# Column mean of an 8192 x 8192 matrix: other early blocks, an earlier start for TensorE's sums, two GpSimd adds and stores from two queues

## The chip, the cores and the metric

The kernel runs on one core of a Trainium2 chip. The metric is device time in microseconds (us): the median of three runs. Engines are named as the profile names them: PE is TensorE, DVE is VectorE, ACT is ScalarE, POOL is GpSimd, SP is SyncE. Times inside the profiled execution are counted from the start of its span.

## The reference

```python
def setup_inputs():
    return {
        "x": np.random.randn(8192, 8192).astype(np.float32),
    }

def reference(x: np.ndarray) -> np.ndarray:
    return np.mean(x, axis=0)
```

The input is 268.4 MB, the output 32 KB.

## The kernel before

**Tiling.** The 8192 rows are G = 64 groups of 128 rows, so a group is a tile of 128 partitions by 8192 float32 (4096 KB). Columns are cut into 16 blocks of F = 512; the sixteenth block is cut once more into four quarters of W = 128. The sum over the 64 groups and 128 partitions is made in two stages: VectorE adds groups element by element into `acc`, and TensorE sums over the partitions by a matmul with a 128 x 32 tile `ones` that holds 1/8192, adding up in PSUM what it is given: `acc` and the last two groups (62 and 63), which VectorE never touches.

**Loads.** All are issued by SyncE, in program order, through `load` (L52). `early` (6 blocks wide) is filled with the first six blocks of group 61 (`load_early`, L88: two blocks at once, four more at g = 4). Groups come in pairs, 8192 KB per load (L98), into four buffers `bufs[:, 0:4]` (and the first pair into the two that become `both` and `acc`). After the loop come group 60, the last ten blocks of group 61, group 62, and group 63 in four pieces of 8, 4, 3 and 1 blocks (L117 to L122). A load that reuses a buffer waits for the VectorE add that read it.

**VectorE.** For each pair, one add makes `both` from the pair (L106) and one adds `both` to `acc` (L107); then group 60 (all 16 blocks, L117) and group 61 (its last ten blocks, L119) are added to `acc`. In `add` (L71) an add that waits for a load has its waits put on a no-op of another engine's queue, ScalarE's or GpSimd's (L75), and waits for that no-op alone.

**GpSimd** adds the six early blocks to `acc`, in two adds, after g = 24 and g = 32 (L111).

**TensorE.** `blocks` (L126) lists one matmul per block: block i goes to strip q = i % 4, that is output partitions 32q to 32q + 31 of PSUM tile `banks[i // 4]`; the quarters of block 15 go to the four strips of `last`. The order is fixed by hand: all of group 62, all of `acc`, all of group 63 (L135 to L137), 16 blocks each. In the profile each matmul stands as two records: 90 records for 45 blocks, 24 for 12 quarters.

**Output.** ScalarE copies the four banks to SBUF (L152), VectorE copies `last` to `tail` (L160), and SyncE stores: banks 0 to 2 in one store, bank 3 in a second, `tail` in a third (L164 to L166). `landed` (L46) makes SyncE wait for what must be over by the end.

Of the kernel before, what the change touches and what calls it, by code (L numbers as in the profile page):

```python
# [9 lines left out]
def kernel(  # L10
# [5 lines left out]
    nc = tc.nc  # L16
    f32 = mybir.dt.float32
    M, N = x.shape
    P = nc.NUM_PARTITIONS
    F = 512  # L20
    W = F // 4
    G = M // P
# [8 lines left out]
    acc = bufs[:, U - 1, :]  # L31
    ones = sb.tile([P, 32], f32, name="ones")
    E = 6
    early = sb.tile([P, E * F], f32, name="early")
# [6 lines left out]
    banks = [psp.tile([P, F], f32, name=f"bank{b}") for b in range(4)]  # L41
# [4 lines left out]
    def landed(*inss):  # L46

        nop = tc.keep_in_program_order(nc.sync.nop()).ins
        for o in inss:
            tc.add_manual_dep(nop, o.name, sync, reason="SyncE waits")  # L50

    def load(dst, src):  # L52
        ins = tc.keep_in_program_order(nc.sync.dma_start(out=dst, in_=src)).ins  # L53
        k = len(loads)
        over = loads[k - 8:k - 6] if k >= 8 and k % 2 == 0 else []
        tc.declare_no_dep(ins, group="loads", keep=over, reason="the reader of the buffer waited")
        for o in over:
            tc.add_manual_dep(ins, o.name, sync, reason="covers the next load too")
        tc.add_to_no_dep_group("loads", ins)
        loads.append(ins)  # L60
        return ins

    def rows(g, n=1):
        return x[g * P:(g + n) * P, :]
# [6 lines left out]
    def add(dst, a, b, dmas):  # L71

        ins = tc.keep_in_program_order(nc.vector.tensor_add(out=dst, in0=a, in1=b)).ins  # L73
        if dmas:
            waiter = nc.scalar if len(adds) % 8 > 1 else nc.gpsimd  # L75
            nop = joins[waiter] = tc.keep_in_program_order(waiter.nop()).ins  # L76
            for o in dmas + adds[-1:]:
                tc.add_manual_dep(nop, o.name, sync, reason="the no-op waits")
            for group in ("loads", "adds"):
                tc.declare_no_dep(ins, group=group, reason="the no-op waited")  # L80
            tc.add_manual_dep(ins, nop.name, sync, reason="waits for both at once")
        elif adds:
            tc.declare_no_dep(ins, group="loads", reason="the add ahead waited")
        tc.declare_no_dep(ins, group="early", reason="the no-op waited, or the add behind it")
        tc.add_to_no_dep_group("adds", ins)
        adds.append(ins)

    def load_early(lo, hi):  # L88
        load(early[:, lo * F:hi * F], rows(G - 3)[:, lo * F:hi * F])

    sums2 = bufs[:, U - 2:, :]
    load_early(0, 2)
    first = [load_rows(0, U - 2, 2)]
    tc.keep_in_program_order(nc.scalar.copy(out=warm[:], in_=ones[:]))  # L94
    ahead = []
    for g in range(2, G - 4, 2):
        u = (g + 2) % 4
        dma = load_rows(g, u, 2)  # L98
        if g < 6:
            add(sums2, sums2, bufs[:, u:u + 2, :], [dma] + first)  # L100
            first = []
            if g == 4:
                load_early(2, E)
                add(acc, acc, both, [])
            continue
        add(both, bufs[:, u, :], bufs[:, u + 1, :], [dma])  # L106
        add(acc, acc, both, ahead)  # L107
        ahead = []
        if g in (24, 32):
            cols = slice(0, 2 * F) if g == 24 else slice(2 * F, E * F)  # L110
            ins = tc.keep_in_program_order(nc.gpsimd.tensor_add(  # L111
                out=acc[:, cols], in0=acc[:, cols], in1=early[:, cols])).ins
            tc.add_to_no_dep_group("early", ins)
            ahead = [ins]

    r60, r61, r62, r63 = [bufs[:, (G - 4 + 2 + j) % 4, :] for j in range(4)]
    add(acc, acc, r60, [load(r60, rows(G - 4))])  # L117
    cols = slice(E * F, N)
    add(acc[:, cols], acc[:, cols], r61[:, cols], [load(r61[:, cols], rows(G - 3)[:, cols])])  # L119
    load(r62, rows(G - 2))  # L120
    for lo, hi in [(0, 8), (8, 12), (12, 15), (15, 16)]:
        load(r63[:, lo * F:hi * F], rows(G - 1)[:, lo * F:hi * F])  # L122

# [2 lines left out]
    def blocks(row, lo, hi):  # L126
        for i in range(lo, hi):
            if i < 15:
                sums.append((banks[i // 4], i % 4, row[:, i * F:(i + 1) * F]))
            else:  # L130
                for q in range(4):
                    at = i * F + q * W
                    sums.append((last, q, row[:, at:at + W]))

    blocks(r62, 0, 16)  # L135
    blocks(acc, 0, 16)
    blocks(r63, 0, 16)  # L137
    for n, (dst, q, cols) in enumerate(sums):
        summed = tc.keep_in_program_order(nc.tensor.matmul(  # L139
            out=dst[32 * q:32 * q + 32, :],  # L140
            lhsT=ones[:],
            rhs=cols,
            start=all((d is dst, k) != (True, q) for d, k, _ in sums[:n]),
            stop=all((d is dst, k) != (True, q) for d, k, _ in sums[n + 1:]),
            tile_position=(0, 32 * q),
            skip_group_check=True,
        )).ins

    res = both[:, :4 * F].rearrange("p (b c) -> p b c", b=4)

    def copy(dst, src):
        return tc.keep_in_program_order(nc.scalar.copy(out=dst, in_=src)).ins  # L152

    def store(engine, dst, src):
        return tc.keep_in_program_order(engine.dma_start(out=dst, in_=src)).ins

    for b in range(3):
        copy(res[:, b, :], banks[b][:])
    copied = copy(res[:96, 3, :], banks[3][:96])
    ended = nc.vector.tensor_copy(out=tail[:], in_=last[:]).ins  # L160
    landed(*joins.values())
    landed(loads[-5], set_up)
    landed(*loads[-4:-2])
    s0 = store(nc.sync, out[:12 * F].rearrange("(b q c) -> q b c", q=4, c=F), res[0:P:32, 0:3, :])  # L164
    s3 = store(nc.sync, out[12 * F:15 * F].rearrange("(q c) -> q c", q=3), res[0:96:32, 3, :])
    store(nc.sync, out[15 * F:].rearrange("(q c) -> q c", q=4), tail[0:P:32, :])  # L166
    landed(*loads[-2:])
    landed(copied, summed)
    landed(s0, ended)
    landed(s3)  # L170
    hold = tc.keep_in_program_order(nc.vector.nop()).ins
    tc.add_manual_dep(hold, s0.name, sync, reason="VectorE ends late")
# [30 lines left out]
```

## Time and profile before

| what | value |
|---|---|
| time, median of three runs (lowest to highest) | 631.97 us (631.57 to 632.15) |
| the profiled execution: its own time | 632.94 us |
| the profiled execution: its span | 630.8 us |
| HBM read / written | 268.44 MB / 0.03 MB, 426 GB/s over the span |
| busy in the span: DVE / PE / POOL / ACT | 529.8 / 14.0 / 7.4 / 3.8 us |
| group 62 and later loads issued by SyncE from | 596.14 us |
| TensorE's matmuls, first start to last end | 612.97 to about 627 us |

Sections of the page: 1 gives busy time by engine, 2 the span in 40 slices, 4 the chain of work that ended last, 5 groups of instructions by line. "SPq" and "ACTq" are the sequencers of SyncE and ScalarE; a DMA issue there is the time that the issuing takes, not the transfer. Over most of the span the DMA rows are full; the last 20 us are where the engines' order shows.

### The profile page before, as it was taken

The page shows a single profiled execution, that of the slowest core. Times are in us where ns is not written, and L with a number is a line of the kernel's source. Part 1 is how long each engine was busy: PE and PEld are TensorE (multiplying, and loading weights), DVE is VectorE, ACT ScalarE, POOL GpSimd, SP SyncE. Part 2 cuts the span into 40 slices and gives each one's busy share as a digit, 9 for nine tenths or more (in the row PEclk, how much of TensorE's full clock was granted, in tenths as well). Part 3 has the DMA queues.
Part 4 walks back from the last instruction along what each step waited for, and adds up shares of the span by engine and source line. Part 5 has one row for each costly group of instructions (what it writes and reads, how often), then busy time and mean ns, then how long its engine had stood idle before and what let it go on. Part 6 is the DMA issues. An engine that isn't in the chain of part 4 may idle for free.

```text
span 630.8 us, 448 instructions
## 1 busy us (share of the span) xinstructions
PE 14.0 (2%) x114; PEld 5.3 (1%) x114; DVE 529.8 (84%) x60; ACT 3.8 (1%) x6; POOL 7.4 (1%) x8
## 2 busy tenths in 40 slices
PE   0000000000000000000000000000000000000017
PEld 0000000000000000000000000000000000000002
DVE  0028999999888898888998899988889888889892
ACT  0000000000000000000000000000000000000001
POOL 0000000000000000010000200000000000000000
PEclk9999999999999999999999999999999999999999
DMA  9999999999999999999999999999999999999994
GB/s 387 445 449 390 479 411 461 403 465 399 465 399 465 399 465 399 465 399 465 399 465 411 453 420 445 441 424 449 416 461 403 461 403 465 399 465 399 422 430 182
DMA packets 5648, 268.50 MB, mean 426 GB/s; under 512 B 635, under 2 KB 639, under 8 KB 1038
## 3 DMA queue, kind: packets, MB, share of 16 engines
q1 hardware_dynamic: 5646, 268.47, 98.5%
q8 instruction: 1, 0.02, 0.0%
q14 instruction: 1, 0.01, 0.0%
HBM read 268.44 MB, written 0.03 MB: 426 GB/s over the span
## 4 chain that ended last, share of the span: by engine, by line
DMA 66%; DVE 28%; another core or an unknown queue 3%; PE 2%; issue 0%; SPq 0%; ACT 0%; ACTq 0%; POOLq 0%
DMA bufs<-in_x_dram 66%; DVE bufs L73 28%; PE bank L139 2%; SPq L53 0%; PE last L139 0%; ACT bufs L152 0%; ACTq L76 0%; POOLq L76 0%
## 5 line engine op out<-in xcount | busy, mean ns | idle before, releaser
L73 DVE TENSOR_TENSOR bufs<-bufs 128x8192 f32<-128x8192 f32 (+2 forms) x59 | 529.5, 8975 | 89.7 <-POOLq L76 54.0
L139 PE MATMUL bank<-bufs,ones 128*32 128x512 f32 x90 | 13.8, 729 | 613.0 <-DMA bufs<-in_x_dram 613.0
L111 POOL TENSOR_TENSOR bufs<-bufs,early 128x1024 f32<-128x1024 f32 (+1 forms) x2 | 6.8, 3416 | 349.9 <-DVE bufs L73 349.9
L139 PEld LDWEIGHTS bank<-bufs,ones 128*32 128x32 f32 x90 | 4.7, 129 | 619.4 <-issue 617.9
L160 DVE COPY tail<-last 128x128 f32<-128x128 f32 x1 | 0.3, 292 | 7.8 <-PE bank L139 7.8
L152 ACT COPY bufs<-bank 128x512 f32<-128x512 f32 (+1 forms) x4 | 2.3, 585 | 622.8 <-PE bank L139 622.8
L139 PE MATMUL last<-bufs,ones 128*32 128x128 f32 x24 | 2.7, 287 | 0.0
L94 ACT ACT_TABLE_LOAD x1 | 1.3, 1283 | 0.7 <-PEq L187 0.7
L139 PEld LDWEIGHTS last<-bufs,ones 128*32 128x32 f32 x24 | 1.2, 112 | 2.0 <-issue 2.0
L94 ACT COPY warm<-ones 128x32 f32<-128x32 f32 x1 | 0.2, 217 | 0.0
L40 POOL TENSOR_TENSOR ready<-ones 128x1 f32<-128x1 f32 x1 | 0.2, 193 | 0.1
L37 POOL MEMSET ones<- 128x32 f32 x1 | 0.1, 124 | 0.3 <-POOLq L187 0.3
L187 POOL MEMSET const-bfloat16-1.0<- 128x1 bf16 x1 | 0.1, 101 | 0.0
L187 POOL MEMSET const-uint8-127<- 128x1 uint8 x1 | 0.1, 101 | 0.0
L187 POOL MEMSET const-float32-0.0<- 128x1 f32 x1 | 0.1, 98 | 0.2 <-issue 0.2
L187 POOL MEMSET const-float32-1.0<- 128x1 f32 x1 | 0.1, 98 | 0.0
## 6 DMA issues: line engine op xcount, KB each, us to landing
bufs<-in_x_dram SPq DMA_DIRECT2D x2, 4096.0 KB, 16.7
bufs<-in_x_dram SPq DMA_DIRECT2D x1, 2560.0 KB
bufs<-in_x_dram SPq DMA_DIRECT2D x1, 2048.0 KB, 21.3
early<-in_x_dram SPq DMA_DIRECT2D x1, 1024.0 KB, 62.3
bufs<-in_x_dram SPq DMA_DIRECT2D x1, 1024.0 KB, 23.2
bufs<-in_x_dram SPq DMA_DIRECT2D x1, 768.0 KB, 24.7
early<-in_x_dram SPq DMA_DIRECT2D x1, 512.0 KB
bufs<-in_x_dram SPq DMA_DIRECT2D x30, 29.9
```

The lines of the kernel that those rows point to most:

```text
L37: nc.gpsimd.memset(ones[:], 1.0 / M)
L40: nc.gpsimd.tensor_add(out=ready[:], in0=ones[:, 0:1], in1=ones[:, 1:2])).ins
L73: ins = tc.keep_in_program_order(nc.vector.tensor_add(out=dst, in0=a, in1=b)).ins
L94: tc.keep_in_program_order(nc.scalar.copy(out=warm[:], in_=ones[:]))
L111: ins = tc.keep_in_program_order(nc.gpsimd.tensor_add(out=acc[:, cols], in0=acc[:, cols], in1=early[:, cols])).ins
L139: summed = tc.keep_in_program_order(nc.tensor.matmul(out=dst[32 * q:32 * q + 32, :], lhsT=ones[:], rhs=cols, start=all((d is dst, k) != (T ...
L152: return tc.keep_in_program_order(nc.scalar.copy(out=dst, in_=src)).ins
L160: ended = nc.vector.tensor_copy(out=tail[:], in_=last[:]).ins
L187: nc = _bacc.Bacc("TRN2", target_bir_lowering=False, num_devices=1)
```

## The change

Four things are changed; the loop over pairs stays.

1. `early` now holds the first six blocks of group 60 instead of 61. So after the loop the load of group 60 brings its last ten blocks and the load of group 61 all sixteen, and VectorE adds ten blocks of each (128 x 5120 twice instead of 128 x 8192 and 128 x 5120).
2. The first six blocks of group 61 are summed elsewhere: blocks 0 and 1 are added to `acc` by GpSimd (`join(r61, 0, 2)`), blocks 2 to 5 go to TensorE. A second GpSimd add takes blocks 6 and 7 of group 62 into `acc` (`join(r62, 6, 8)`).
3. TensorE's order is new: six blocks of `acc`, four of group 61, fourteen of group 62, and so on, as the diff has it. Block and strip of each matmul are as before.
4. ScalarE stores bank 0 after its copy, and bank 3 after its copy; SyncE stores banks 1 and 2, and `tail`.

```diff
     def load_early(lo, hi):
-        load(early[:, lo * F:hi * F], rows(G - 3)[:, lo * F:hi * F])
+        load(early[:, lo * F:hi * F], rows(G - 4)[:, lo * F:hi * F])
...
     r60, r61, r62, r63 = [bufs[:, (G - 4 + 2 + j) % 4, :] for j in range(4)]
-    add(acc, acc, r60, [load(r60, rows(G - 4))])
     cols = slice(E * F, N)
-    add(acc[:, cols], acc[:, cols], r61[:, cols], [load(r61[:, cols], rows(G - 3)[:, cols])])
+    for row, g, lo in [(r60, G - 4, E * F), (r61, G - 3, 0)]:
+        add(acc[:, cols], acc[:, cols], row[:, cols], [load(row[:, lo:], rows(g)[:, lo:])])
+
+    def join(row, lo, hi):
+        at = slice(lo * F, hi * F)
+        return tc.keep_in_program_order(nc.gpsimd.tensor_add(
+            out=acc[:, at], in0=acc[:, at], in1=row[:, at])).ins
+
+    join(r61, 0, 2)
     load(r62, rows(G - 2))
+    joined = join(r62, 6, 8)
...
-    blocks(r62, 0, 16)
-    blocks(acc, 0, 16)
-    blocks(r63, 0, 16)
+    blocks(acc, 0, 6)
+    blocks(r61, 2, 6)
+    blocks(r62, 0, 6)
+    blocks(r62, 8, 16)
+    blocks(acc, 8, 16)
+    blocks(r63, 0, 4)
+    blocks(acc, 6, 8)
+    blocks(r63, 4, 16)
...
-    for b in range(3):
+    copy(res[:, 0, :], banks[0][:])
+    s0 = store(nc.scalar, out[:4 * F].rearrange("(q c) -> q c", q=4), res[0:P:32, 0, :])
+    for b in (1, 2):
         copy(res[:, b, :], banks[b][:])
     copied = copy(res[:96, 3, :], banks[3][:96])
+    s3 = store(nc.scalar, out[12 * F:15 * F].rearrange("(q c) -> q c", q=3), res[0:96:32, 3, :])
     ended = nc.vector.tensor_copy(out=tail[:], in_=last[:]).ins
...
-    s0 = store(nc.sync, out[:12 * F].rearrange("(b q c) -> q b c", q=4, c=F), res[0:P:32, 0:3, :])
-    s3 = store(nc.sync, out[12 * F:15 * F].rearrange("(q c) -> q c", q=3), res[0:96:32, 3, :])
+    s1 = store(nc.sync, out[4 * F:12 * F].rearrange("(b q c) -> q b c", q=4, c=F), res[0:P:32, 1:3, :])
     store(nc.sync, out[15 * F:].rearrange("(q c) -> q c", q=4), tail[0:P:32, :])
     landed(*loads[-2:])
-    landed(copied, summed)
-    landed(s0, ended)
+    landed(joined, copied)
+    landed(s0, summed)
+    landed(s1, ended)
     landed(s3)
```

In the built program TensorE's first matmul waits for the first `join`; on GpSimd's queue that `join` stands behind the no-op that waits for group 60's load and for the last add of the loop, and behind two more waiting instructions; the second `join` waits for VectorE's last add.

## The prediction

> **What bounds the kernel now.** I read the page first: slices, then the chain of waits.
>
> ```profile
> span 630.8 us, 448 instructions
> ...
> PE   0000000000000000000000000000000000000017
> ...
> DMA  9999999999999999999999999999999999999994
> ...
> DMA bufs<-in_x_dram 66%; DVE bufs L73 28%; PE bank L139 2%; SPq L53 0%; PE last L139 0%; ACT bufs L152 0%; ACTq L76 0%; POOLq L76 0%
> ```
>
> The DMA row is full in 39 of 40 slices: 268 MB come in at one pace, and the change moves none of these bytes. Only the last slice, where DMA falls and PE rises, can give or lose time. The table of windows shows where the input ends (columns: PE, PEld, DVE, ACT, POOL busy; granted clock; DMA share; GB/s), and the chain in order of time what follows:
>
> ```profile
> 621.00:622.00 1.00, 1.00 (x12) 0.37 (x7) 0.00 (x0) 0.00 (x0) 0.00 (x0) 1.00 0.88 340
> 622.00:623.00 1.00, 1.00 (x16) 0.36 (x13) 0.00 (x0) 0.00 (x0) 0.00 (x0) 1.00 0.06 21
> ```
> ```profile
> 596.14 16.73 DMA bufs<-in_x_dram
> 612.88 0.09 issue
> 612.97 5.56 PE bank L139 x25
> ```
>
> The input is in at about 622.1, yet the span ends at 630.8. The chain goes by the load of group 62 (in at 612.88) and then by TensorE without a pause: the end is TensorE's 14 us of sums behind group 62. The timeline shows its pace and what comes behind it (start, duration):
>
> ```profile
> 604.95 8.69 DVE L73 TENSOR_TENSOR bufs<-bufs 128x8192 f32<-128x8192 f32 x1
> 613.74 5.49 DVE L73 TENSOR_TENSOR bufs<-bufs 128x5120 f32<-128x5120 f32 x1
> ...
> 618.85 0.61 PE L139 MATMUL bank<-bufs,ones 128*32 128x512 f32 x3
> ...
> 622.11 0.41 PE L139 MATMUL last<-bufs,ones 128*32 128x128 f32 x2
> 622.51 0.61 PE L139 MATMUL bank<-bufs,ones 128*32 128x512 f32 x3
> ...
> 626.16 0.61 PE L139 MATMUL bank<-bufs,ones 128*32 128x512 f32 x3
> ...
> 626.82 0.58 ACT L152 COPY bufs<-bank 96x512 f32<-96x512 f32 x1 [0.26 <-PE bank L139]
> 627.06 0.29 DVE L160 COPY tail<-last 128x128 f32<-128x128 f32 x1 [7.82 <-PE bank L139]
> ...
> 628.30 0.56 SPq L155 DMA_DIRECT2D out_dram<-tail  x1
> ```
>
> The three-matmul rows (blocks 12 to 14 of group 62, of acc, of group 63) are 3.66 and 3.65 us apart: a group of 16 blocks costs 3.65 us. Group 62 itself took from 612.97 to 619.3, some 6.3 us; there the matmuls last 1.06 us instead of 0.59, so TensorE runs at half pace for its first 5.8 us, though the granted clock reads 1.00 throughout. Four strips work side by side: a strip has four blocks of each group, so one block costs its strip about 0.85 us (3.65 less 0.24 for the quarters, by four).
>
> **Early blocks of 60 (edit 1).** Same bytes, same number of loads, same buffers: 0 for the stream. VectorE's add of group 60 shrinks from 8.69 to 5.49 us and would end at 604.95 + 5.49 = 610.44. It gives nothing by itself: TensorE needs acc's upper blocks later than that. Its cover would be gone if TensorE caught up with VectorE (second rival).
>
> **Where TensorE starts (edit 2).** Its first matmul now waits for the first GpSimd add, and 50 block sums queue behind it. What does that add cost, and when does it run? The trace has two such adds; this is the second:
>
> ```profile
> 353.34 4.49 POOL L111 TENSOR_TENSOR bufs<-bufs,early 128x2048 f32<-128x2048 f32 x1 [75.07 <-DVE bufs L73]
> 355.20 11.18 DVE L73 TENSOR_TENSOR bufs<-bufs 128x8192 f32<-128x8192 f32 x1 [1.94 <-ACTq L76]
> ```
>
> A two-block add took 2.34 us (at 275.93). But look at VectorE: its add, started 1.86 us into GpSimd's, took 11.18 instead of 8.69 us: 2.49 more, for an overlap of 2.63. After GpSimd's end it needs 8.55 us, its whole work. The two don't run together: the later one stands still. There GpSimd was first, since VectorE waited for a load. In the change both are let go by one event, the end of the last acc add at 604.84. VectorE starts 0.10 us after it, through GpSimd's own no-op; the join stands behind that no-op and behind two more waits, a few hundredths each (the no-op and waits in the trace last 0.02 to 0.05 us, with gaps of the same size), so at about 605.0 to 605.1. VectorE is first, by my estimate, and GpSimd waits for its 5.49 us. Between VectorE's two adds there is a gap of 0.10 us (604.84 to 604.95 shows one); I let GpSimd in there, since VectorE, held up, went on without a measurable delay. Bounds: the join ends at 605.05 + 2.34 = 607.4 if it doesn't wait, at 612.8 in the gap (610.44 + 2.34), at 618.3 if it waits for both adds (615.95 + 2.34). I take 612.8, by the rows above. TensorE then starts at 612.85, where it did before: **-0.1 us**. VectorE's second add is held until 612.8 and ends at 618.3 (before: 619.23); the second join ends at 620.7. TensorE's 24 blocks ahead of acc's upper half last past 619, so both are covered.
>
> [...]
>
> **TensorE's load (edit 3).** 50 blocks instead of 48, but unevenly: strip 0 gets acc 0, 4; r61 4; r62 0, 4, 8, 12; acc 8, 12; r63 0, 4, 8, 12 = 13, where it had 12. Thirteen times 0.85 for twelve: **+0.85 us**. Bounds: +0.43 (two blocks at a quarter of 0.85 each, were strips balanced) and +1.7 (two half-filled rounds, behind r61 5 and r62 5, were strips unable to run ahead). I take +0.85, because the row at 622.11 shows two matmuls of the quarters running ahead of blocks issued before them. [...]
>
> **Stores (edit 4).** Before, the tail store is ready at 627.35 (627.06 + 0.29) but issued at 628.30, behind two others. After, SyncE has only banks 1 and 2 ahead of it, and it goes at about 627.4; bank 3 goes from ScalarE at the same time. The end then follows bank 3's store, whose issue (0.78, by the store line's longest row) is 0.2 longer than the tail's (0.56): 0.95 - 0.08 - 0.21 = **-0.65 us**. Bounds: -0.87 if both land as the tail's did; +0.78 if ScalarE's issuing, which the trace doesn't show, puts a further issue of that length on the way. I take -0.65: bank 0's store is issued while TensorE still has ten blocks to do.
>
> **Sum.** -0.1 + 0.85 - 0.65 = +0.1 us on a span of 630.8, which is 632.94 + 0.1 for that execution; it stands 0.97 over the median 631.97, so **632.1 us**. Own range of this case: 631.97 - 0.1 + 0.43 - 0.87 - 0.3 = 631.1 to 631.97 - 0.1 + 1.7 + 0.4 = 634.0 (0.3 is half the spread of the runs before; 0.4 some of the ScalarE bound).
>
> **Rivals.** *GpSimd isn't held up* (it gets in first, or shares): join at 607.4, and TensorE does ten blocks before group 62 is in. VectorE, held by the join if the two exclude each other, ends at 618.3, and from there strips need acc 8 to 15 (1.9), r63 0 to 3 (0.85), then strip 2 acc 6, r63 6, 10, 14 (3.4) and a quarter (0.2): 624.7 plus 0.3 to drain, against 627.06. That is -2.1, with the stores -2.75: 629.2. With no exclusion at all VectorE is done at 616, strip 2 ends by 623.7, and -4.0 gives 628.0. For it: no row shows GpSimd waiting. Against: the start times above. I put it at 629.0.
>
> *GpSimd is starved* (slower): it misses the 0.10 us gap at 610.44, waits for VectorE's second add, and ends at 618.3. TensorE, whose first instruction waits for it, starts 5.4 us late with everything still to do: +5.4 + 0.85 - 0.65 = +5.6, 637.6. [...] For it: TensorE's first wait has no way round. Against: 0.10 us is ample by the 8.55 us above.
>
> *The stream ends it anyway*: group 63's last piece is in at 622.1 and needs only a block and a store; no case gets below about 627.5.
>
> **Numbers.** Forecast 0.55, not held up 0.28, starved 0.17. What a measurement can tell is 0.2%, 1.3 us: below 630.7 is faster, above 633.2 slower. Of the forecast's 0.55 I give 0.04 to faster and 0.12 to slower (strips in order). Faster 0.32, same 0.39, slower 0.29. The range takes in the forecast and the case of no hold-up: 628.3 to 634.0; starved is left out.
>
> **What would show it.** GpSimd's first added line: start and length (2.3 from 605, about 7.8 from 605, or two adds long); VectorE's adds at 604.95 and behind; TensorE's first matmul (607.5, 612.9 or 618.4); strips' pace of 3.65 us per 16 blocks; the tail store's issue right behind its copy. The forecast is wrong if TensorE starts by 608.

## The result, and the profile after

| kernel | median (lowest to highest) | runs |
|---|---|---|
| before | 632.15 us (631.57 to 633.01) | 17 |
| after | 632.99 us (632.10 to 634.72) | 17 |

The ratio is 1.0017, 95% interval 1.0010 to 1.0025: 0.8 us slower by the medians. The interval leaves out 1, so the change costs a little time, but the ratio is inside the 0.2% that was called no change. The profiled execution of the changed kernel has a span of 631.5 us, 0.77 us more than before. Its page, slices:

```profile
span 631.5 us, 464 instructions
...
PE   0000000000000000000000000000000000000017
...
POOL 0000000000000000010000200000000000000041
...
DMA  9999999999999999999999999999999999999994
```

The DMA row is as it was; what is new is GpSimd's work in the last two slices. The chain of waits in order of time (start, duration, what):

```profile
596.33 16.50 DMA bufs<-in_x_dram
...
612.88 7.72 PE bank L152 x43
```

And the timeline, with VectorE's two adds first, then the other engines:

```profile
605.13 5.49 DVE L73 TENSOR_TENSOR bufs<-bufs 128x5120 f32<-128x5120 f32 x1
...
610.73 7.44 DVE L73 TENSOR_TENSOR bufs<-bufs 128x5120 f32<-128x5120 f32 x1
```
```profile
605.39 7.43 POOL L123 TENSOR_TENSOR bufs<-bufs 128x1024 f32<-128x1024 f32 x1 [247.34 <-DVE bufs L73]
...
612.88 8.01 PE L152 MATMUL bank<-bufs,ones 128*32 128x512 f32 x44 [612.88 <-POOL bufs L123]
...
618.25 2.37 POOL L123 TENSOR_TENSOR bufs<-bufs 128x1024 f32<-128x1024 f32 x1 [5.43 <-DVE bufs L73]
...
625.02 1.13 ACTq L168 DMA_DIRECT2D out_dram<-bufs  x1
...
627.61 0.58 ACT L165 COPY bufs<-bank 96x512 f32<-96x512 f32 x1 [0.26 <-PE bank L152]
627.84 0.29 DVE L176 COPY tail<-last 128x128 f32<-128x128 f32 x1 [9.67 <-PE bank L152]
628.19 0.56 SPq L168 DMA_DIRECT2D out_dram<-tail  x1
628.22 0.72 ACTq L168 DMA_DIRECT2D out_dram<-bufs  x1
```

Read it in order. VectorE's add of group 60 starts at 605.13, GpSimd's first join at 605.39. VectorE takes its normal 5.49 us; the join takes 7.43, which is VectorE's remaining 5.23 and 2.2 of its own. Then the roles turn: VectorE's second add starts at 610.73, inside the join, and takes 7.44. The second join, with VectorE idle, takes 2.37. TensorE's first matmul is released by the join, at 612.88, where it was released by group 62's load before (612.97). So the early start does not happen, and TensorE has 50 blocks behind that point instead of 48. The copy of `tail` starts at 627.84 instead of 627.06.

A number that the page's granted clock row (1.00 throughout) doesn't give comes from the matmul records: they last 1.06 us until 618.8 before the change, until 617.4 after it, then 0.59. Counting the half-pace stretch half, TensorE's work from its first matmul to the start of `tail`'s copy was 5.82/2 + 8.27 = 11.18 us before and 4.54/2 + 10.43 = 12.70 after. This is the measure of "work" below. It repeats from profile to profile: with TensorE's order of the kernel before it is 11.18 again in run 9, with the changed order 12.70 again in run 3, though the half-pace stretch is shorter in both (4.35 and 4.31 us).

The end of TensorE's work shows where the two orders differ. Before (first fence), the last six records, of three strips, end together; after (second fence), one strip still has half a block and its quarter to do when the others end:

```profile
626.59 0.40 PE L139 MATMUL last<-bufs,ones 128*32 128x128 f32 x6
```
```profile
626.56 0.56 PE L152 MATMUL last<-bufs,ones 128*32 128x128 f32 x6
626.98 0.59 PE L152 MATMUL bank<-bufs,ones 128*32 128x512 f32 x1
627.41 0.38 PE L152 MATMUL last<-bufs,ones 128*32 128x128 f32 x2
```

A record doesn't name its strip. By the order of issue the late one is strip 2: its block 14 of group 63 is the last whole block.

### The profile page after: what moved, and what is told of

It reads as the page before. It is cut to its first block, busy times and chain, and to the rows that moved or that the text cites. A ratio compares the mean times of both kernels' runs of the same rounds, so it can differ in the third digit from the quotient of the medians.

```text
span 631.5 us, 464 instructions
## 1 busy us (share of the span) xinstructions
PE 14.9 (2%) x118; PEld 5.7 (1%) x118; DVE 528.5 (84%) x60; ACT 3.8 (1%) x6; POOL 17.2 (3%) x10
## 4 chain that ended last, share of the span: by engine, by line
DMA 66%; DVE 28%; another core or an unknown queue 3%; PE 2%; issue 0%; SPq 0%; ACT 0%; ACTq 0%; POOLq 0%
DMA bufs<-in_x_dram 66%; DVE bufs L73 28%; PE bank L152 2%; SPq L53 0%; PE last L152 0%; ACT bufs L165 0%; ACTq L76 0%; POOLq L76 0%
## 5 line engine op out<-in xcount | busy, mean ns | idle before, releaser
L123 POOL TENSOR_TENSOR bufs<-bufs 128x1024 f32<-128x1024 f32 x2 | 9.8, 4902 | 252.8 <-DVE bufs L73 252.8
L152 PEld LDWEIGHTS bank<-bufs,ones 128*32 128x32 f32 x94 | 4.7, 124 | 620.2 <-POOL bufs L123 612.9
```

The costliest lines, as they stand in the source:

```text
L123: return tc.keep_in_program_order(nc.gpsimd.tensor_add(out=acc[:, at], in0=acc[:, at], in1=row[:, at])).ins
L152: summed = tc.keep_in_program_order(nc.tensor.matmul(out=dst[32 * q:32 * q + 32, :], lhsT=ones[:], rhs=cols, start=all((d is dst, k) != (T ...
```

## The experiments

Each was timed beside the kernel before on the same chip; ratios are to that kernel. Edits are against the changed kernel unless said otherwise.

**1. GpSimd goes first.**

```diff
-    for row, g, lo in [(r60, G - 4, E * F), (r61, G - 3, 0)]:
-        add(acc[:, cols], acc[:, cols], row[:, cols], [load(row[:, lo:], rows(g)[:, lo:])])
...
+    l60 = load(r60[:, E * F:], rows(G - 4)[:, E * F:])
+    l61 = load(r61, rows(G - 3))
     join(r61, 0, 2)
+    add(acc[:, cols], acc[:, cols], r60[:, cols], [l60])
+    add(acc[:, cols], acc[:, cols], r61[:, cols], [l61])
```

> The first GpSimd add is put ahead of the no-op that releases VectorE's add of group 60; nothing else moves. Theory (the two engines exclude each other and the later one stands still): GpSimd's add runs alone from 605.1, 2.3 us long; VectorE's add of group 60 ends at 612.8 either way; TensorE starts at 607.5 and does its first ten blocks before group 62 is in, waits for VectorE's second add until about 618.4, and ends at about 625, 2.8 us earlier than in the changed kernel: 630.2 us, about 0.997 of the kernel before. Rival (GpSimd's add is slow at this place for a reason of its own, such as the loads running beside it): it lasts about 7 us again, TensorE starts at 612 to 613, and the time stays at 632 to 633, ratio 1.001 to 1.002.

Measured: 630.65 us, ratio 0.9970 (0.9959 to 0.9982). Its timeline:

```profile
605.13 2.34 POOL L120 TENSOR_TENSOR bufs<-bufs 128x1024 f32<-128x1024 f32 x1 [247.12 <-DVE bufs L73]
605.19 7.63 DVE L73 TENSOR_TENSOR bufs<-bufs 128x5120 f32<-128x5120 f32 x1 [0.20 <-POOLq L76]
...
607.53 1.94 PE L153 MATMUL bank<-bufs,ones 128*32 128x512 f32 x8 [607.53 <-POOL bufs L120]
```

The same two instructions, 0.06 us apart in the other order, and the whole stall changes sides: 2.34 instead of 7.43 for GpSimd, 7.63 instead of 5.49 for VectorE. Nothing is slow about the place. What the hold-up costs is 5.35 us of TensorE's start, and that is worth 0.0047 of the time, some 3 us, and not all 5.35, since TensorE later waits for VectorE (1.54 us, from 616.9 to 618.5).

**2. TensorE begins with what needs no join.**

```diff
-    blocks(acc, 0, 6)
+    blocks(acc, 2, 6)
     blocks(r61, 2, 6)
     blocks(r62, 0, 6)
     blocks(r62, 8, 16)
+    blocks(acc, 0, 2)
     blocks(acc, 8, 16)
```

> TensorE's two blocks that need GpSimd's add (blocks 0 and 1 of acc) are moved behind group 62; the add itself stays where it is and is held up as before. Theory (what costs is that TensorE's first instruction waits for the join): TensorE starts at 604.9, does eight blocks by 608.4, goes on at 612.9 with group 62 at half pace, and ends 1.7 to 2.1 us before the changed kernel: about 631.0 us, 0.998 to 0.999 of the kernel before. Rival (TensorE's end is set by something behind the join, such as VectorE's later end or GpSimd's second add): 633, ratio 1.0015.

Measured: 631.72 us, ratio 0.9992 (0.9983 to 1.0000). The join is held up as before (605.05, 7.43 us), TensorE starts at 604.83, and 0.0025 of the time, 1.6 us, comes back: the wait at the head of TensorE's queue is what costs. By windows, TensorE alone (busy, matmuls, granted clock, DMA share, GB/s):

```profile
604.00:612.50 8.50, 3.64 (x16) 0.98 0.94 405
612.50:616.00 3.50, 3.23 (x19) 0.57 1.03 440
```

After eight blocks TensorE stands still for 4.30 us until group 62 is in, and then the granted clock is 0.57 over the first 3.5 us. The row above it reads 0.98, but all sixteen records ahead of the gap last 1.06 us: these matmuls had run at half pace too. The trace has the full clock from 608.66, when TensorE had just stopped, to 612.08, and half from there to 615.49. So it came up only as TensorE stopped and fell back in the gap. That is the half pace which was expected at group 62.

**3. Stores as before.**

```diff
-    copy(res[:, 0, :], banks[0][:])
-    s0 = store(nc.scalar, ...)
-    for b in (1, 2):
+    for b in range(3):
         copy(res[:, b, :], banks[b][:])
...
-    s3 = store(nc.scalar, ...)
...
-    s1 = store(nc.sync, ...)
+    s0 = store(nc.sync, ...)
+    s3 = store(nc.sync, ...)
...
```

> The changed kernel with its stores as in the kernel before: three, all by SyncE. Forecast's view (the four stores save 0.65 us): 0.65 us slower than the changed kernel, 633.6, ratio 1.0025 to 1.003. Theory now (in the changed kernel's profile the span ends 3.4 us after the copy of tail, as before, so the four stores save nothing): no difference from the changed kernel, 633.0, ratio 1.0010 to 1.0020.

Measured: 633.28 us, ratio 1.0019 (1.0010 to 1.0027), against 1.0017 (1.0010 to 1.0025) with the four stores: no difference that could be told. In the profiles the span ends this long after the copy of `tail` has ended: 3.43 us before, 3.42 after, 3.36 here, 3.1 to 3.3 in runs 1, 2, 4 and 5. So the new stores bring between nothing and 0.3 us.

**4. Group 62's blocks in an order that fills the strips.**

```diff
-    blocks(r62, 0, 6)
-    blocks(r62, 8, 16)
+    blocks(r62, 2, 4)
+    blocks(r62, 0, 2)
+    blocks(r62, 10, 12)
+    blocks(r62, 4, 6)
+    blocks(r62, 14, 15)
+    blocks(r62, 8, 10)
+    blocks(r62, 12, 14)
+    blocks(r62, 15, 16)
```

> The changed kernel with the same 50 blocks for TensorE and the same first blocks, but group 62's blocks in an order in which neighbours lie on different strips. Theory (a strip cannot run far ahead, so the two half-filled rounds behind blocks 5 of groups 61 and 62 cost 0.85 us each at full pace): TensorE needs 0.6 to 0.9 us less, 632.3 us, ratio 1.000 to 1.001. Forecast's view (each strip goes its own way, and strip 0's thirteen blocks set the end whatever the order): no difference, 633.0, ratio 1.0010 to 1.0020.

Measured: 633.54 us, ratio 1.0015 (1.0006 to 1.0024). TensorE's work is 4.94/2 + 10.23 = 12.70 us, the same, and one strip ends alone as in the changed kernel. The half-filled rounds only move: rounds in which two records start instead of four begin at 617.7 in the changed kernel and at 619.9 here. The theory that filling them in group 62 saves time falls.

**5. TensorE without acc's blocks 6 and 7.**

```diff
     blocks(r63, 0, 4)
-    blocks(acc, 6, 8)
     blocks(r63, 4, 16)
```

> The changed kernel without TensorE's two matmuls of acc's blocks 6 and 7 (the sums of columns 3072 to 4095 are left incomplete); both GpSimd adds stay. Theory (strips are in step again when group 63's turn comes, so that strip 2, which has five blocks from there on, sets the end, and the count is nine rounds by strip 0 and five by strip 2): one round less, 0.85 us at full pace, 632.1 us; TensorE's work, with the half-pace stretch counted half, falls from 12.7 to 11.8 us. Forecast's view (strip 0's thirteen blocks set the end, and acc 6 and 7 lie on strips 2 and 3): no difference, 12.7 us, 633.0.

Measured: 632.52 us, ratio 1.0009 (1.0000 to 1.0018). TensorE's work is 4.40/2 + 9.86 = 12.06 us: 0.64 less, though neither block lies on strip 0. So in the changed kernel strip 0's count does not set the end; strip 2's, with block 6 of acc among group 63's, does. Without it two strips end together, and none is left alone. The changed kernel's records show what "in step" means: two strips start group 63 at 623.10 and 623.12, the other two at 623.30, though strip 2 has had seven blocks by then and strip 0 nine. By the count of its blocks, it stood in the rounds in which only two records start. Why it did not use that time to run further ahead stays open.

**6. The first join dropped.**

```diff
-    join(r61, 0, 2)
...
-    blocks(acc, 0, 6)
-    blocks(r61, 2, 6)
+    blocks(r61, 0, 6)
+    blocks(acc, 0, 6)
```

> The changed kernel without its first GpSimd add: TensorE takes blocks 0 to 5 of group 61 itself, ahead of acc's first six. Theory (the join's hold-up is all that keeps TensorE from an early start): TensorE starts at 603.4, when group 61 is in, and has done twelve blocks when group 62 is in at 612.9; VectorE's adds take 5.5 us each and end at 616; TensorE then follows the loads, with 0.5 to 1 us of lag, and ends at about 624: 629 us, ratio 0.995. Rival (something else, such as VectorE's end or the half-pace stretch, holds TensorE): above 631.

Measured: 630.40 us, ratio 0.9973 (0.9964 to 0.9983). TensorE starts at 603.17, and VectorE's adds take 5.49 us each, but TensorE ends at 624.7, not 624. By windows, TensorE alone:

```profile
612.50:616.00 3.50, 3.17 (x22) 0.74 1.05 449
616.00:619.00 3.00, 3.00 (x27) 0.74 0.93 391
```

Again the clock goes after the gap before group 62 (3.98 us here, until 612.83): the trace has it at half from 614.17 to 617.58.

**7. No joins behind the loop**: TensorE takes all of group 61, and VectorE adds group 60 alone.

```diff
-    for row, g, lo in [(r60, G - 4, E * F), (r61, G - 3, 0)]:
-        add(acc[:, cols], acc[:, cols], row[:, cols], [load(row[:, lo:], rows(g)[:, lo:])])
...
-    join(r61, 0, 2)
+    add(acc[:, cols], acc[:, cols], r60[:, cols], [load(r60[:, cols], rows(G - 4)[:, cols])])
+    load(r61, rows(G - 3))
     load(r62, rows(G - 2))
-    joined = join(r62, 6, 8)
...
-    blocks(acc, 0, 6)
-    blocks(r61, 2, 6)
...
-    blocks(r63, 4, 16)
+    blocks(r61, 0, 16)
+    blocks(acc, 0, 16)
+    blocks(r62, 0, 16)
+    blocks(r63, 0, 16)
```

> No GpSimd add behind the loop: TensorE takes all of group 61 (16 blocks from 603.4), then acc, group 62 and group 63, 64 blocks in all; VectorE adds only group 60's last ten blocks and ends at 610.4. Theory: all but the last group is done by 616.6, TensorE ends 0.6 to 1 us behind the last load (622.8), and the span ends 3.1 to 3.4 us after that: about 628.6 us, ratio 0.9945. Rival (16 more blocks make TensorE the bound, or its clock falls back in the gaps between the loads and it runs at half pace at the end): 630 to 632.

Measured: 630.57 us, ratio 0.9974 (0.9964 to 0.9985); 2 us of the gain are missing. The timeline:

```profile
619.30 1.93 PE L140 MATMUL bank<-bufs,ones 128*32 128x512 f32 x16 [2.23 <-DMA bufs<-in_x_dram]
...
623.65 1.06 PE L140 MATMUL bank<-bufs,ones 128*32 128x512 f32 x6 [0.81 <-DMA bufs<-in_x_dram]
```

TensorE waits for each of the four pieces of group 63 some 1.5 us longer than the piece needed in other runs, which accounts for 1.5 of the 2 us. The trace has sixteen landings for a load: fifteen come by 617.7, 620.2, 622.1 and 622.7, the last one at 619.25, 621.74, 623.61 and 624.24. The DMA queues between 616 and 619.5 (packets, MB, share of 16 engines) have what the changed kernel's have not in that window:

```profile
q8 instruction: 1, 0.02, 1.8%
```

One instruction transfer of 16 KB, at 616.59, 1.02 us long. In the kernel before it comes at 623.56, when the input is in.

**8. Padding behind TensorE's last sum**, to move that transfer: run 7 and

```diff
+    spare = psp.tile([32, 32], f32, name="spare")
...
+    for n in range(24):
+        tc.keep_in_program_order(nc.tensor.matmul(
+            out=spare[:], lhsT=ones[:], rhs=ones[:, :32], start=True, stop=True,
+            tile_position=(0, 0), skip_group_check=True))
```

> The kernel without joins, with 24 small matmuls (32 columns, into a spare PSUM tile that nobody reads) behind TensorE's last sum. In the run without them the 16 KB instruction transfer came at 616.6, among the loads of group 63, instead of at 622 to 623.6 as in all other runs, and one of the sixteen landings of each of the four pieces then came 1.5 us behind the rest. Theory (that transfer is triggered by how few instructions TensorE has left, and takes its DMA engine from the loads): it comes after 622.5, group 63's pieces land whole at 617.8, 620.3, 622.2 and 622.8, and the end is 1.0 to 1.5 us earlier: 629.3 us, ratio 0.995 to 0.996. Rival (the late landings are a chance of that one execution, or the transfer's time hangs on the start of the program): the transfer and the time stay, 630.5, ratio 0.997 to 0.998.

Measured: 630.78 us, ratio 0.9978 (0.9969 to 0.9987). The transfer comes at 616.96, and the late landings stay (619.12, 621.45, 623.30, 623.94). They are no chance of one execution, and the count of what TensorE has left is not the trigger: that theory falls.

**9. The same padding on the kernel before.**

> The kernel before with the same 24 small matmuls behind its last sum, as a control: they lie behind everything that the output waits for, so the time stays at that of the kernel before (ratio 0.999 to 1.001) if TensorE's own end does not set the span's; the 16 KB transfer moves from 623.6 to 625 or later. If the small matmuls cost time by themselves, the ratio is above 1.002.

Measured: 632.01 us, ratio 0.9998 (0.9988 to 1.0007); the transfer at 623.27, not later as was expected. The padding costs nothing, and moves nothing that could be told.

**10. Run 6 with the gap filled** by four matmuls of 512 columns, on one strip, behind the first twelve blocks.

```diff
+    spare = psp.tile([32, F], f32, name="spare")
...
     for n, (dst, q, cols) in enumerate(sums):
+        if n == 12:
+            for k in range(4):
+                tc.keep_in_program_order(nc.tensor.matmul(
+                    out=spare[:], lhsT=ones[:], rhs=early[:, :F], start=True, stop=True,
+                    tile_position=(0, 0), skip_group_check=True))
```

> The kernel with the first join dropped, with four matmuls of 512 columns behind TensorE's first twelve blocks, on one strip, into a spare PSUM tile that nobody reads: 3.4 us of work for the gap from 608.9 to 612.8 in which TensorE waited for group 62, and behind which the granted clock fell to half from 614.2 to 617.6. Theory (that gap is what takes the clock away, and half pace costs half of 3.4 us there): the clock stays at 1.00 from about 607.5 on, TensorE ends at 623.7 to 624.0 instead of 624.7, and the time is 0.6 to 1.0 us lower: 629.6 us, ratio 0.9955 to 0.9965. Rival (TensorE's end follows VectorE, GpSimd and the loads there, whatever its clock): no difference, ratio 0.997 to 0.998.

Measured: 630.29 us, ratio 0.9968 (0.9956 to 0.9980). By windows the clock now stays:

```profile
612.50:616.00 3.50, 2.99 (x28) 1.00 1.02 435
616.00:619.00 3.00, 3.00 (x38) 1.00 0.96 401
```

But the time hardly moves, because something else takes its place (timeline):

```profile
623.28 1.06 PE L157 MATMUL bank<-bufs,ones 128*32 128x512 f32 x6 [1.24 <-DMA bufs<-in_x_dram]
```

The instruction transfer has come forward to 620.05, and the last landings of group 63's last two pieces are at 623.23 and 623.87, a microsecond behind the other fifteen. So the theory of the clock is right here (0.74 with the gap in run 6, 1.00 without it), and the gain goes in the wait for a late landing. That the transfer makes it late is argued from runs 7, 8 and 10, which alone have both; no run moved the transfer on purpose.

**11. Run 1 with group 63's first eight blocks ahead of acc's upper half.**

```diff
-    blocks(acc, 8, 16)
-    blocks(r63, 0, 4)
-    blocks(acc, 6, 8)
-    blocks(r63, 4, 16)
+    blocks(r63, 0, 8)
+    blocks(acc, 8, 16)
+    blocks(acc, 6, 8)
+    blocks(r63, 8, 16)
```

> The kernel with the join first, with the first eight blocks of group 63 moved ahead of acc's upper half in TensorE's order. There TensorE stood idle from 616.9 to 618.5 for VectorE's second add, which the join had held up, while these blocks were in at 617.9. Theory (that wait is the price of letting GpSimd go first): TensorE goes on at 618.0 and ends 0.5 us earlier than 625.15, 630.1 us, ratio 0.996 to 0.9965. Rival (the number of rounds on strip 2 behind that point sets the end, and seven of them stay): no difference, 630.65, ratio 0.997.

Measured: 630.00 us, ratio 0.9967 (0.9955 to 0.9980), the lowest median of all. `tail`'s copy starts at 624.68 instead of 625.17. TensorE goes on at 617.98, after 1.04 us. The interval overlaps run 1's, so the 0.5 us rest on the two profiles; that the kernel beats both before and after does not hang on them.

## Why the prediction was right

The measured 632.99 us lies in the range of 631.1 to 634.0, and what was forecast happens: no early start, and a time that hardly moves. Two of the four terms were as worked out; the other two were too low, both in the same direction.

**The stream unchanged (edit 1): right.** Group 62 is in at 613.08 in the changed kernel, 612.88 before; the DMA rows are the same.

**The join is held up and gets in between VectorE's adds: right.** Predicted: from 605.0 to 605.1, end 612.8, VectorE's second add to 618.3, second join to 620.7. Measured: 605.39, 612.82, 618.17, 620.62. Both directions of the exclusion are now in rows; before, only one was. In the kernel before, VectorE's add that started inside GpSimd's took 11.18 us instead of 8.69; here the join that started inside VectorE's add took 7.43 instead of the second join's 2.37. Run 1, with the two starts in the other order (2.34 us for the join, 7.63 for VectorE's add), shows that this order is the cause.

**TensorE starts where it did: right.** 612.88, a difference of -0.09 for the predicted -0.1.

**TensorE's load: right in sign, mis-sized.** The term was "+0.85", by strip 0's thirteen blocks. Measured 12.70 - 11.18 = 1.5 us, near the upper bound of 1.7. It has two parts. Run 5, in which strip 2 no longer ends last, needs 12.06 us, 0.88 more than before: that agrees with the thirteenth block as forecast. The other 0.64 is acc's blocks 6 and 7, which were counted as free on strips 2 and 3: strip 2, with twelve blocks, ends after strip 0 with thirteen. The reason given for the upper bound is not the right one, since run 4 shows that the order inside group 62 does nothing. Running ahead, which the row of the quarters showed, does not reach as far as the forecast took it; how far it reaches stays open.

**Stores: wrong.** The term was "-0.65"; measured -0.01 between the two profiles, no difference in run 3. SyncE does issue `tail`'s store at once, 0.06 us after its copy instead of 0.95, and bank 3's goes beside it. But the last landing of `tail`'s store comes 2.57 us after the issue started, where it was 1.62 before (2.29 in run 1). Only one of its four pieces is late: three have landed by 629.82, the fourth at 630.76. An instruction transfer of 8 KB falls among them, from 629.41 to 629.72 (DMA queues, 629.3 to 629.8):

```profile
q14 instruction: 1, 0.01, 3.9%
```

The fourth piece starts at 629.72, where it ends; the other three had started by 629.42. The thirteen profiles divide the same way: in the nine in which such a transfer runs just ahead of or among the pieces, the last landing comes 0.7 to 0.9 us behind the others; in the four in which it comes later (before, runs 3 and 9) or is over 0.6 us before the pieces start (run 5), it comes 0.05 behind them at most. Run 5 has ScalarE's store beside it too, so that store alone does not make `tail`'s late. That the transfer does is argued from these profiles; no run moved it on purpose. An estimate from the rows: without the late landing, bank 3's store, in at 630.28, would have come last, 2.14 us after `tail`'s copy, against 2.57 for the last landing before, so the four stores would have saved some 0.4 us and not 0.65.

**The sum.** +0.1 was predicted. The two misses have one sign: by the terms as measured, -0.09 + 1.5 - 0.01 = +1.4. Between the two profiled executions it is 0.77, because the half-pace stretch was 1.3 us shorter after the change, worth 0.65. In the medians it is 0.84; how long the stretch was in the executions without a profile is not known, so what takes up the rest there stays open. That the forecast missed the median by no more than 0.9 us, with its two misses adding up, is in part luck. The stretch was 4.3 to 5.8 us long in the profiles in which TensorE started at 612.7 to 613.1, so the spans of two profiles can't settle a term of this size; the measure of work can, and the bounds of the forecast covered both misses.

**The rivals.** *GpSimd isn't held up* is run 1: 630.65 where 629.2 was worked out and 629.0 put. TensorE's part came out: `tail`'s copy starts at 625.17, and 625.0 was worked out. The stores save 0.3 instead of 0.65. The rest is in how the sum was taken: the 627.06 that these times were set against stands in an execution 0.97 us over the median, and the saving was then taken from the median. *GpSimd is starved* didn't happen: a gap of about 0.1 us between two VectorE adds (610.62 to 610.73) was enough. *The stream ends it* came about in runs 7, 8 and 10 alone, where TensorE's last matmuls wait for late pieces of group 63.

## What to carry to other kernels

In these runs a small add given to GpSimd beside VectorE's long adds cost one of the two engines the other's time (7.43 us instead of 2.37 for the join in the changed kernel, 7.63 instead of 5.49 for VectorE's add in run 1), and which one was settled by who started first: put the one that others wait for first in its queue, or don't let the head of a queue wait for it. Work moved to the front of an engine's queue is worth only what the first wait there lets through (with the join at the head TensorE started at 612.88, without it in run 2 at 604.83); read that wait before counting instructions. When two terms are a few tenths of a microsecond, compare work with the clock taken out, and expect the next limit (here a late landing of a load, a wait of 1.24 us in run 10) just behind the one removed.

## What the runs showed of the hardware that was not expected

- TensorE's granted clock fell back with a gap before the last loads: with 4.30 us of standing still (run 2) and 3.98 (run 6) it fell to half for 3.4 us, in run 2 still in the gap, in run 6 1.3 us after it; after 2.23 (run 7) and 1.54 (run 1) the next matmuls went on at full pace (their weight loads come 0.43 us apart), and filling the gap (run 10) kept the clock at 1.00. Run 8 was at half pace again (0.86 us apart) after 2.02 us, so the length of the gap alone doesn't decide.
- In the three runs in which an instruction transfer of 16 KB, about 1 us long, fell well before the last loads were in (616.6 in run 7, 617.0 in run 8, 620.05 in run 10), one of the sixteen landings of the loads behind it was 1.0 to 1.6 us late; in the other ten profiles it came at 621.9 or later, and no last landing was more than 0.3 us behind the one before it. It came when TensorE had started 76 to 81 matmul records in the kernels that start at 612.7 or later, and 94 to 114 in those that start earlier and wait for loads; padding at the end did not move it forward or back by more than 0.4 us (616.96 in run 8 against 616.59 in run 7, 623.27 in run 9 against 623.56 before). What sets its moment stays open.
